# Parts of q and k kept in DRAM in the order of the contraction's rows, in a two-layer trunk of four mixers on one core

## The chip, the cores and the metric

The kernel runs on one core of one Trainium2 chip. A core has a matmul engine (PE, whose weight loads are listed as PEld), a vector engine (DVE), a scalar engine (ACT), a general one (POOL) and a queue of its own for transfers (SP, listed as SPq). Each engine works through its own list of instructions in order and waits at an instruction until everything that it needs is there. The transfers of SP are carried by 16 DMA engines. The metric is the time of the whole program on the device in microseconds (us); lower is better.

## The reference

One step of a hybrid trunk: DEPTH = 2 layers over 1024 latent tokens and 128 context tokens, width 1024. Cut to what the change touches:

```python
# in each layer: one input projection, four mixers, one output projection, then an MLP
nq, nk = rms_norm(heads(nq), g), rms_norm(heads(nk), g)           # 4 heads of 64
y_nat = nat_latent_attend(nq, nk, nv, nat_kc, nat_vc, rel_bias)   # windows of the 16 x 64 grid + 256 cached keys
dq, dk = rms_norm(halves(dq), g), rms_norm(halves(dk), g)         # 4 heads of 2 x 32
dq, k_all = axial_rope(dq), concat([diff_kc, axial_rope(dk)])     # 256 cached keys first
y_diff = rms_norm(softmax(q1 @ k1.T) @ v - lam * softmax(q2 @ k2.T) @ v)
mixed = concat([y_ssd, y_nat, y_rwkv, y_diff])
x = x + g1 * (mixed @ w_out)
x = x + g2 * (square(relu(norm(x) @ w_ff1)) @ w_ff2)
```

## The kernel before

Tokens lie along the free dimension: an activation is a tile of 128 features by T = 1152 tokens, and keys have 256 cached columns more (1408). Every matmul operand of the projections is split in two parts, `h` (rounded) and `l` (the rest), so that three products give the accuracy of float32. The scores of the attentions use the same split in one product: the contraction's rows hold the h part and the l part of the same features side by side.

A layer runs through these stages: norm and projections with the SSD mixer beside them; the projections of q and k (`proj_qk`) beside the first step of the RWKV mixer; the neighbourhood attention (`nat_core`) and then the differential attention (`diff_core`) beside the rest of RWKV; the output projection; the MLP. A scheduler orders the instructions of every engine when the program is built, by its own estimate of times, so an edit in one place can move instructions far from it.

In `split_to` the finished q or k of a chunk is copied to `qh` by ACT, the rest `ql` is taken by POOL, and SP writes both to a scratch tensor in DRAM: `nscr` for the neighbourhood attention, `dscr` for the differential one, both of shape [4 (q of two feature tiles, k of two), 2 parts, 128 features, 1408]. The tiles `qh` and `ql` have two buffers each, so the third write of a kind needs the first to have landed.

`nat_core` goes through four heads of 64 features. For each it fills `Q` (128 rows: 64 of part h, then 64 of part l) and two tiles `K0`, `K1` (128 rows each: 64 rows of one part of k, twice), with one transfer for every block of 64 rows: six transfers. `diff_core` goes through four heads, each of two halves; for each half `diff_operands` fills `Q` and `K` with one transfer for every block of 32 rows: four and four, the rows of Q being h, h, l, l and those of K h, l, h, l. All these tiles have one buffer for each tag, so the transfers for the next head wait until the last product `S` of the head before has read the tile, and the first `S` of the next head waits until they have landed. I call this place a head change; there are three in each attention of each layer, twelve in all. A ninth block of tokens (`b == 8`, the context) is the last of each head. What PE has to do between the two products is work of the block before (transposes at L1154, products with V at L1166) and of RWKV (L935 to L986).

Where `nat_core` begins, SP also carries the loads `vv`, `z` (the RWKV state) and the triangle blocks `Ti` to DRAM and back as `D`, and DVE has RWKV's short steps on `D` (L866 to L873) in the same list as the reading of the scores (L1279).

Of the kernel before, what the change touches and what calls it, by code (L numbers as in the profile page):

```python
# [8 lines left out]
F32 = mybir.dt.float32  # L9
# [8 lines left out]
NS, NP_ = 1024, 128  # L18
T = NS + NP_
# [11 lines left out]
def bcast_mid(ap, n):  # L31
    return ap.unsqueeze(1).to_broadcast([ap.shape[0], n, ap.shape[1]])
# [988 lines left out]

def split_to(env, tp, x, n, dst, c0, grid=False):

    nc = env.nc
    h = tp.tile([128, 384], F32R, tag="qh", name="qh", bufs=2)
    l = tp.tile([128, 384], F32R, tag="ql", name="ql", bufs=2)
    if grid:
        m = min(NS - c0, n)
        parts = [(by_columns(x[:, :m]), slice(0, m), lambda a: a.rearrange("p (b r c) -> p b r c", b=8, c=8))]
        if m < n:  # L1030
            parts.append((x[:, m:n], slice(m, n), lambda a: a))
        for xv, s, f in parts:
            nc.scalar.activation(out=f(h[:, s]), in_=xv, func=AF.Copy)
            nc.gpsimd.tensor_tensor(out=f(l[:, s]), in0=xv, in1=f(h[:, s].bitcast(F32)), op=ALU.subtract)
        g0 = c0 // 8
        for part, t in ((0, h), (1, l)):
            nc.sync.dma_start(out=dst[part][:, 0:NS].rearrange("p (b x) -> p b x", b=8)[:, :, g0:g0 + m // 8], in_=t[:, :m].bitcast(F32).rearrange("p (b x) -> p b x", b=8))
            if m < n:
                nc.sync.dma_start(out=dst[part][:, NS:T], in_=t[:, m:n].bitcast(F32))
        return  # L1040
    nc.scalar.activation(out=h[:, :n], in_=x, func=AF.Copy)
    nc.gpsimd.tensor_tensor(out=l[:, :n], in0=x, in1=h[:, :n].bitcast(F32), op=ALU.subtract)
    nc.sync.dma_start(out=dst[0][:, c0:c0 + n], in_=h[:, :n].bitcast(F32))
    nc.sync.dma_start(out=dst[1][:, c0:c0 + n], in_=l[:, :n].bitcast(F32))


class Steps:
# [87 lines left out]
    steps.add(last, turn, scale, *([] if rope is None else [rotate]))  # L1135


def cached_keys(env, tp, ck, scr):
    for t in range(2):
        x = tp.tile([128, 384], F32, tag="qx", name="cx", bufs=7)  # L1140
        env.nc.sync.dma_start(out=x[:, 0:256], in_=ck[t])
        split_to(env, tp, x[:, 0:256], 256, scr[2 + t], T)


def pv(env, sp, ps, e, kt, V, r0):
# [61 lines left out]
def nat_core(env, ps, pss, scr, vsrc, cv, nbias, yout, beside):  # L1207

    tc, nc, C = env.tc, env.nc, env.const
    with ExitStack() as ctx:  # L1210
        big = ctx.enter_context(tc.tile_pool(name="na_big", reuse_waits="tile", bufs=1, side="right"))
        sp = ctx.enter_context(tc.tile_pool(name="na_s", reuse_waits="tile", bufs=2, side="right"))
        behind, steps = Behind(), Steps()
# [16 lines left out]
        for h in range(4):  # L1230
            t, r0 = h // 2, (h % 2) * 64
            if h % 2 == 0:
                y = big.tile([128, T], F32, tag="y", name="nay", bufs=2)
            Q = sp.tile([128, T], F32R, tag="Q", name="Q", bufs=1)
            K = [sp.tile([128, T + 256], F32R, tag=f"K{i}", name=f"K{i}", bufs=1) for i in range(2)]

            for a in range(2):
                nc.sync.dma_start(out=Q[a * 64:a * 64 + 64].bitcast(F32), in_=scr[t, a, r0:r0 + 64, 0:T])
                for i in range(2):
                    nc.sync.dma_start(out=K[i][a * 64:a * 64 + 64].bitcast(F32), in_=scr[2 + t, i, r0:r0 + 64])  # L1240
            if r0 == 0:
                V = sp.tile([128, 11, 128], F32, tag="V", name="V", bufs=1)
                nc.sync.dma_start(out=V[:, 0:9], in_=vsrc[:, :, h * 64:h * 64 + 128])
                nc.sync.dma_start(out=V[:, 9:11], in_=cv[:, :, h * 64:h * 64 + 128])

            BT = sp.tile([128, 3, 16, 24], F32, tag="BT", name="BT", bufs=1)
            for m in range(3):
                nc.sync.dma_start(out=BT[:, m].rearrange("p a k -> p (a k)"), in_=nbias[:, m, :, h])
            BI = sp.tile([128, 9, 16, 8], F32, tag="BI", name="BI")
            nc.gpsimd.memset(BI[:, 2:4], 0.0)  # L1250
            for m, (o, i, n) in enumerate(((0, 1, 2), (4, 0, 2), (6, 0, 3))):
                nc.gpsimd.tensor_copy(BI[:, o:o + n], BT[:, m, :, i * 8:i * 8 + n * 8].rearrange("p a (b k) -> p b a k", b=n))
            flat = BI.rearrange("p b a k -> p (b a k)")
            if h == 1:
                beside()
            for b in range(NB):
                q = Q[:, b * 128:b * 128 + 128]

                if b == 8:
                    segs, kt = [([(NS, 128)], flat[:, 256:384])], [8]  # L1260
                elif b == 0:
                    segs, kt = [([(0, 256), (T, 256)], flat[:, 0:512])], [0, 1, 9, 10]
                elif b == 7:
                    segs, kt = [([(T, 256), (768, 256)], flat[:, 256:768])], [9, 10, 6, 7]
                else:
                    segs, kt = [([(b * 128 - 128, 384)], flat[:, 768:1152]), ([(T, 256)], flat[:, 256:512])], [b - 1, b, b + 1, 9, 10]
                kt = [(k, 128, i * 128) for i, k in enumerate(kt)]
                st = sp.tile([128, 8], F32, tag="st", name="st", bufs=4)
                e = sp.tile([128, 640], F32, tag="e", name="e", bufs=3)

                o = 0
                for i, (seg, bias) in enumerate(segs):
                    S = pss.tile([128, 512], F32, tag="s", name="S")
                    w = 0
                    for k0, n in seg:
                        nc.tensor.matmul(S[:, w:w + n], q, K[0][:, k0:k0 + n], start=True, stop=False)
                        nc.tensor.matmul(S[:, w:w + n], q, K[1][:, k0:k0 + n], start=False, stop=True)
                        w += n
                    nc.vector.tensor_tensor_reduce(out=e[:, o:o + w], in0=S[:, 0:w], in1=bias, op0=ALU.add, op1=ALU.min,  # L1279
                                                   scale=-1.0, scalar=st[:, 0:1] if i else 3e38, accum_out=st[:, i:i + 1])  # L1280
                    o += w
                nc.scalar.activation(out=e[:, 0:o], in_=e[:, 0:o], func=AF.Exp, scale=-1.0, bias=st[:, len(segs) - 1:len(segs)], accum_out=st[:, 4:5])
                nc.vector.reciprocal(out=rec[:, t, b, h % 2:h % 2 + 1], in_=st[:, 4:5])

                def values(b=b, h=h, e=e, kt=kt, V=V, y=y, r0=r0):
                    o = pv(env, sp, ps, e, kt, V, r0)
                    if b < 8:
                        nc.vector.tensor_copy(by_columns(y[r0:r0 + 64, 0:NS])[:, b], o.rearrange("p (r c) -> p r c", c=8))
                    else:
                        nc.vector.tensor_copy(y[r0:r0 + 64, NS:T], o)  # L1290
                    steps()
                    if r0 and b in (3, 7, 8):
                        steps.add(lambda: scale(h // 2, b // 4 * 4, 1 if b == 8 else 4, y))

                behind(values)
# [5 lines left out]
def diff_operands(env, pool, scr, j):  # L1301

    t, q0 = j // 4, (j % 4) * 32
    Q = pool.tile([128, T], F32R, tag=f"Q{j % 2}", name="Q", bufs=1)
    K = pool.tile([128, T + 256], F32R, tag=f"K{j % 2}", name="K", bufs=1)

    for a in range(2):
        for i in range(2):
            r = slice(a * 64 + i * 32, a * 64 + i * 32 + 32)
            env.nc.sync.dma_start(out=Q[r].bitcast(F32), in_=scr[t, a, q0:q0 + 32, 0:T])  # L1310
            env.nc.sync.dma_start(out=K[r].bitcast(F32), in_=scr[2 + t, i, q0:q0 + 32])
    return Q, K


# [111 lines left out]
def kernel(ctx: ExitStack, tc: tile.TileContext, A: dict, O: dict):  # L1426
    nc = tc.nc
    env = Env()
# [4 lines left out]
    def dram(shape):  # L1433
        cnt[0] += 1
        return tc.dram_tile(shape, F32, name=f"scr{cnt[0]}")
# [45 lines left out]
    for L in range(DEPTH):  # L1481
# [2 lines left out]
        zdt, nv, dv = dram([128, NB, 264]), dram([128, NB, 256]), dram([128, NB, 256])  # L1484
        Y = [dram([128, T]) for _ in range(6)]
        rscr = [dram([128, T]) for _ in range(13)]
        nscr, dscr, sk, nbias = dram([4, 2, 128, T + 256]), dram([4, 2, 128, T + 256]), dram([3, 8, 60, 24]), dram([16, 3, 8, 4, 384])
        scale_section(env, md, 1, ng[:, L, 0])
        env.wide = False

# [45 lines left out]
        with tc.tile_pool(name="qk", reuse_waits="tile", bufs=1, side="right") as qp:  # L1536
# [9 lines left out]
                nc.sync.dma_start(out=rope[i], in_=A["c_rope"][i])  # L1546
            steps = Steps()
            for t in range(4):
                proj_qk(env, qp, steps, WF[13 + t], H, pt[:, t:t + 1], 64, nscr[t], O["nat_k"][L, t - 2] if t > 1 else None)
            cached_keys(env, qp, A["nat_ck"][L], nscr)  # L1550
            for t in range(4):
                proj_qk(env, qp, steps, WF[17 + t], H, pt[:, 4 + t:5 + t], 32, dscr[t], O["diff_k"][L, t - 2] if t > 1 else None, rope)
            cached_keys(env, qp, A["diff_ck"][L], dscr)
            rwkv_join(env, u, 0, u00, psr)
            env.stg = qp
            proj_tm(env, A["w_in_tm"][L, 2], H, 256, dv, O["diff_v"][L], steps=steps)
# [218 lines left out]
```

## Time and profile before

| | |
|---|---|
| median of 3 runs | 4177.0 us (4174.42 to 4189.47) |
| profiled execution | 4174.25 us, its span 4172.5 us |
| PE busy | 3976.4 us, 95% of the span |
| PEld, DVE, ACT, POOL busy | 3688.6, 2479.1, 1499.7, 1122.7 us |
| mean granted clock of PE | 0.968 of 2.4 GHz |
| share of the 16 DMA engines' time in SP's transfers | 30.4% |

A busy engine is one that has an instruction under way; the granted clock is the share of its full speed that PE was given. The durations that the prediction uses come from the profiled execution, 2.75 us below the median.

### The profile page before, as it was taken

The numbers are of one execution on the slowest core, as the hardware profiler recorded it, in microseconds if no ns is written. First come the engines' busy times: TensorE is split into PE (matmuls) and PEld (weight loads), VectorE is DVE, ScalarE is ACT, GpSimd is POOL, SyncE is SP. The second block draws the span as 40 slices with busy tenths as digits, with TensorE's granted clock in tenths as the row PEclk, the third lists the DMA queues.
The fourth block names the chain that finished last, engine by engine and source line by source line (L and its number), as shares of the span: only waits on it lengthen the run. The fifth ranks groups of instructions, "written<-read, shape, count | busy, mean of one in ns | idle before, by whom it ended". The sixth has DMA issues, their size and how long they took to land.

```text
span 4172.5 us, 68251 instructions
## 1 busy us (share of the span) xinstructions
PE 3976.4 (95%) x26994; PEld 3688.6 (88%) x26994; DVE 2479.1 (59%) x5702; ACT 1499.7 (36%) x2872; POOL 1122.7 (27%) x874
## 2 busy tenths in 40 slices
PE   8899989989999999999999998899999999999999
PEld 5889877867889999999999997687777999999999
DVE  4897657678675994333356647577878363333333
ACT  4323325546643222111244233255567241111111
POOL 2234341123143211111133333302323331121111
PEclk9999989989999999999999999899999999999999
DMA  5654544323131551111135344533122201111112
GB/s 200 203 173 146 134 125 106 79 65 78 46 112 41 162 167 51 44 43 41 41 120 167 121 128 96 153 95 94 32 61 85 99 31 41 41 41 46 41 41 71
DMA packets 259598, 381.81 MB, mean 92 GB/s; under 512 B 123328, under 2 KB 193680, under 8 KB 258256
## 3 DMA queue, kind: packets, MB, share of 16 engines
q1 hardware_dynamic: 259216, 377.44, 30.4%
q8 instruction: 213, 3.49, 0.4%
q14 instruction: 105, 0.86, 0.1%
q0 software_dynamic: 64, 0.02, 0.0%
HBM read 288.43 MB, written 91.50 MB: 91 GB/s over the span
## 4 chain that ended last, share of the span: by engine, by line
PE 74%; DVE 12%; DMA 6%; issue 3%; ACT 2%; SPq 2%; POOL 1%; DVEq 0%; POOLq 0%; ACTq 0%
PE psd L101 12%; PE psd L99 12%; PE psd L100 12%; PE psx L101 5%; PE psx L99 5%; PE psx L100 5%; PE tps L1166 5%; PE tps L1154 2%; PE psd L943 1%; DVE tm L872 1%; PE S L1389 1%; DVE junk L162 1%; PE psd L935 1%; DMA mod<-in_w_mod_dram 1%; DMA Q<-scr 1%
## 5 line engine op out<-in xcount | busy, mean ns | idle before, releaser
L84 POOL TENSOR_TENSOR wl<-raw,wh 128x1024 fp32r<-128x1024 f32 (+3 forms) x200 | 480.0, 2401 | 1524.7 <-ACT wh L82 1513.1
L82 ACT ACTIVATE wh<-raw 128x1024 fp32r<-128x1024 f32 (+3 forms) x200 | 205.8, 1031 | 787.3 <-PE psd L101 667.5
L299 DVE SCALAR_TENSOR_TENSOR x<-psd,md,x 128x384 f32<-128x384 f32 (+2 forms) x442 | 212.7, 504 | 339.4 <-PE psd L101 339.0
L99 PE MATMUL psd<-fh,wl 128*128 128x384 f32 x992 | 334.8, 337 | 0.6 <-DVE s L382 0.6
L101 PE MATMUL psd<-fl,wh 128*128 128x384 f32 x992 | 335.3, 338 | 0.0
L100 PE MATMUL psd<-fh,wh 128*128 128x384 f32 x992 | 334.7, 337 | 0.0
L99 PE MATMUL psd<-h2h,wl 128*128 128x384 f32 x816 | 281.4, 345 | 6.1 <-ACT qx L1122 4.3
L100 PE MATMUL psd<-h2h,wh 128*128 128x384 f32 x816 | 279.4, 343 | 0.0
L101 PE MATMUL psd<-h2l,wh 128*128 128x384 f32 x816 | 278.2, 342 | 0.0
L1166 PE MATMUL tps<-pT,V 128*128 128x128 f32 x1920 | 265.8, 288 | 7.1 <-ACT pT L1161 6.0
L384 DVE TENSOR_TENSOR fl<-s,fh 128x384 fp32r<-128x384 f32 x192 | 207.1, 1079 | 97.4 <-ACT fh L383 97.0
L1166 PEld LDWEIGHTS tps<-pT,V 128*128 128x128 f32 x1920 | 242.1, 200 | 19.9 <-ACT pT L1161 8.2
L99 PE MATMUL psd<-h1h,wl 128*128 128x384 f32 x592 | 204.7, 346 | 8.4 <-ACT st L262 6.4
L99 PE MATMUL psd<-h0h,wl 128*128 128x384 f32 x592 | 206.7, 349 | 2.0 <-ACT st L262 2.0
L382 DVE SCALAR_TENSOR_TENSOR s<-psd,r 128x384 f32<-128x384 f32 x128 | 71.3, 557 | 229.5 <-ACT r L381 229.1
L100 PE MATMUL psd<-h0h,wh 128*128 128x384 f32 x592 | 204.1, 345 | 0.0
L100 PE MATMUL psd<-h1h,wh 128*128 128x384 f32 x592 | 203.8, 345 | 0.0
L101 PE MATMUL psd<-h0l,wh 128*128 128x384 f32 x592 | 203.7, 346 | 0.0
L101 PE MATMUL psd<-h1l,wh 128*128 128x384 f32 x592 | 203.3, 345 | 0.1
L1395 ACT ACTIVATE e<-e,st 128x1280 f32<-128x1280 f32 x144 | 180.6, 1254 | 62.5 <-DVE st L1394 54.2
L1161 ACT ACTIVATE pT<-tps 128x512 f32<-128x512 f32 (+2 forms) x336 | 153.4, 470 | 133.6 <-PE tps L1154 117.0
L299 DVE SCALAR_TENSOR_TENSOR x<-psx,md,x 128x384 f32<-128x384 f32 (+2 forms) x198 | 103.5, 538 | 163.5 <-PE psx L101 163.2
(614 smaller groups left out, 10918.2 us busy)
## 6 DMA issues: line engine op xcount, KB each, us to landing
raw<-in_w_ff_dram SPq DMA_DIRECT2D x128, 512.0 KB
mod<-in_w_mod_dram SPq DMA_DIRECT2D x80, 512.0 KB
raw<-in_w_in_fm_dram SPq DMA_DIRECT2D x42, 512.0 KB
scr<-st SPq DMA_DIRECT2D x78, 192.0 KB
scr<-x SPq DMA_DIRECT2D x26, 576.0 KB
K<-scr SPq DMA_DIRECT2D x32, 352.0 KB
K<-scr SPq DMA_DIRECT2D x64, 176.0 KB
u<-scr SPq DMA_DIRECT2D x18, 576.0 KB
```

The costliest lines, as they stand in the source:

```text
L82: nc.scalar.activation(out=h[:, :n], in_=raw, func=AF.Copy)
L84: nc.gpsimd.tensor_tensor(out=l[:, :n], in0=raw, in1=h[:, :n].bitcast(F32), op=ALU.subtract)
L99: nc.tensor.matmul(ps, al, bh, start=i == 0, stop=False)
L100: nc.tensor.matmul(ps, ah, bh, start=False, stop=False)
L101: nc.tensor.matmul(ps, ah, bl, start=False, stop=i == n - 1)
L299: env.nc.vector.scalar_tensor_tensor(out=x[:, kt, s0:s1], in0=ps[:, s0 - c0:s1 - c0], scalar=g[:, kt, cd:cd + 1], in1=x[:, kt, s0:s1], op0 ...
L382: nc.vector.scalar_tensor_tensor(out=s, in0=ps[:, :n], scalar=0.0, in1=r, op0=ALU.max, op1=ALU.mult)
L384: nc.vector.tensor_tensor(out=fl[j][:, c0:c0 + n], in0=s, in1=fh[j][:, c0:c0 + n].bitcast(F32), op=ALU.subtract)
L1154: nc.tensor.transpose(pp[0:n, i * 128:i * 128 + 128], e[:, o:o + n], C.ident)
L1161: nc.scalar.activation(out=pT[0:g[i][1], i * 128:j * 128], in_=pp[0:g[i][1], i * 128:j * 128], func=AF.Copy)
L1166: nc.tensor.matmul(out, V[0:n, vb], parts[k][0:n], start=k == 0, stop=k == len(kt) - 1)
L1395: nc.scalar.activation(out=e[:, :N], in_=e[:, :N], func=AF.Exp, scale=-1.0, bias=m, accum_out=st[:, 6:7] if c else s0)
```

## The change

The scratch tensors get a new order. `nscr` becomes [4, 128 features, 2 parts, 1408], `dscr` [4, 128 features, 4, 1408]. In `dscr` each part is written twice, next to each other or alternating (q: h, h, l, l; k: h, l, h, l), by one transfer with the source repeated. The rows of a feature then lie in the order in which they are contracted, and `Q` and `K` are each filled by one transfer of 128 rows, in the order feature, part. In `nat_core` the repetition of k's rows is made by the transfer itself. The products, their sizes and their number stay as they are; the order of the rows in a contraction changes for Q and K alike.

```diff
@@ split_to
-        for part, t in ((0, h), (1, l)):
-            nc.sync.dma_start(out=dst[part][:, 0:NS].rearrange("p (b x) -> p b x", b=8)[:, :, g0:g0 + m // 8], in_=t[:, :m].bitcast(F32).rearrange("p (b x) -> p b x", b=8))
+        for d, t in zip(dst, (h, l)):
+            nc.sync.dma_start(out=d[:, 0, 0:NS].rearrange("p (b x) -> p b x", b=8)[:, :, g0:g0 + m // 8], in_=t[:, :m].bitcast(F32).rearrange("p (b x) -> p b x", b=8))
...
-    nc.sync.dma_start(out=dst[0][:, c0:c0 + n], in_=h[:, :n].bitcast(F32))
-    nc.sync.dma_start(out=dst[1][:, c0:c0 + n], in_=l[:, :n].bitcast(F32))
+    for d, t in zip(dst, (h, l)):
+        m = d.shape[1]
+        src = t[:, :n].bitcast(F32)
+        nc.sync.dma_start(out=d[:, :, c0:c0 + n] if m > 1 else d[:, 0, c0:c0 + n], in_=bcast_mid(src, m) if m > 1 else src)
+
+
+def nat_parts(scr, t):
+
+    return scr[t, :, 0:1], scr[t, :, 1:2]
+
+
+def diff_parts(scr, t):
+
+    s = scr[t] if t < 2 else scr[t].rearrange("p (a b) x -> p b a x", a=2)
+    return (s[:, 0:2], s[:, 2:4]) if t < 2 else (s[:, 0], s[:, 1])
@@ nat_core
-            for a in range(2):
-                nc.sync.dma_start(out=Q[a * 64:a * 64 + 64].bitcast(F32), in_=scr[t, a, r0:r0 + 64, 0:T])
-                for i in range(2):
-                    nc.sync.dma_start(out=K[i][a * 64:a * 64 + 64].bitcast(F32), in_=scr[2 + t, i, r0:r0 + 64])
+            nc.sync.dma_start(out=Q.bitcast(F32), in_=scr[t, r0:r0 + 64, :, 0:T].rearrange("f a x -> (f a) x"))
+            for i in range(2):
+                nc.sync.dma_start(out=K[i].bitcast(F32), in_=scr[2 + t, r0:r0 + 64, i].unsqueeze(1).to_broadcast([64, 2, T + 256]))
@@ diff_operands
-    for a in range(2):
-        for i in range(2):
-            r = slice(a * 64 + i * 32, a * 64 + i * 32 + 32)
-            env.nc.sync.dma_start(out=Q[r].bitcast(F32), in_=scr[t, a, q0:q0 + 32, 0:T])
-            env.nc.sync.dma_start(out=K[r].bitcast(F32), in_=scr[2 + t, i, q0:q0 + 32])
+    for X, s, n in ((Q, t, T), (K, 2 + t, T + 256)):
+        env.nc.sync.dma_start(out=X.bitcast(F32), in_=scr[s, q0:q0 + 32, :, 0:n].rearrange("f a x -> (f a) x"))
@@ tile_hybrid_trunk_kernel
-        nscr, dscr, sk, nbias = dram([4, 2, 128, T + 256]), dram([4, 2, 128, T + 256]), dram([3, 8, 60, 24]), dram([16, 3, 8, 4, 384])
+        nscr, dscr, sk, nbias = dram([4, 128, 2, T + 256]), dram([4, 128, 4, T + 256]), dram([3, 8, 60, 24]), dram([16, 3, 8, 4, 384])
```

The callers pass `nat_parts(nscr, t)` or `diff_parts(dscr, t)` where they passed `nscr[t]` or `dscr[t]`. Lines of the new kernel are a few numbers higher (the product S at L1389 is L1398 there).

The scheduler's order differs from the first writes to `dscr` on, in every list of both layers up to the output projection. On SP, where `nat_core` begins in layer 0 (scr_234 is nscr, scr_235 dscr, z_5993 and z_6585 the two states that RWKV needs first), there stood:

```order
L1240 DMA K_8570<-scr_234 64x1408
L1240 DMA K_8571<-scr_234 64x1408
L715 DMA vv<-scr_228 128x1152
L917 DMA z_5993<-in_st_rwkv_dram 128x64
L1238 DMA Q<-scr_234 64x1152
L1240 DMA K_8570<-scr_234 64x1408
L1240 DMA K_8571<-scr_234 64x1408
L1243 DMA V<-scr_213 128x9x128
L1244 DMA V<-in_nat_cv_dram 128x2x128
L1248 DMA BT<-scr_237 128x1x384
L917 DMA z_6585<-in_st_rwkv_dram 128x64
```

Behind these rows SP had two more BT, seven of the eight loads of the first differential half, the two writes of `Ti`, the third z, the eighth load and only then the load of `D`. At the same place there now stands:

```order
L1253 DMA K_8570<-scr_234 128x1x1408
L1253 DMA K_8571<-scr_234 128x1x1408
L1256 DMA V<-scr_213 128x9x128
L1257 DMA V<-in_nat_cv_dram 128x2x128
L715 DMA vv<-scr_228 128x1152
L917 DMA z_5993<-in_st_rwkv_dram 128x64
L1261 DMA BT<-scr_237 128x1x384 x3
L1320 DMA Q<-scr_235 128x1152
L1320 DMA K<-scr_235 128x1408
L917 DMA z_6585<-in_st_rwkv_dram 128x64
L861 DMA scr_5851<-Ti 32x36x32 x2
L917 DMA z_7430<-in_st_rwkv_dram 128x64
```

The load of `D` is the next row. The whole operands and V moved ahead of the first z, and two transfers stand where eight stood ahead of `Ti` and `D`.

On PE, at the last head change of `diff_core` in layer 1 (the first row is the previous head's last product of the first half, the single 128x128 row further down that of the second half; the 128x512 and 128x256 rows are the next head's first products), there stood:

```order
L1389 MATMUL S<-K,Q 128x128
L963 MATMUL psd<-E,R_24967 128x128 x8
L1166 MATMUL tps<-pT,V 128x128 x10
L1389 MATMUL S<-K,Q 128x128
L984 MATMUL psx<-st_24921,E 64x64
L984 MATMUL psx<-st_24924,E 64x64
L986 MATMUL psx<-E,st_24921 64x64
L986 MATMUL psx<-E,st_24924 64x64
L1154 MATMUL tps<-pack,e 128x128 x6
L1389 MATMUL S<-K,Q 128x512
L1389 MATMUL S<-K,Q 128x256
L1389 MATMUL S<-K,Q 128x512
```

And now, with the last product of the first half five rows above the first row shown (four small ones of L984 and L986 lie between):

```order
L957 MATMUL psd<-R_24907,Ti 64x128 x8
L1168 MATMUL tps<-pack,e 128x128 x6
L1398 MATMUL S<-K,Q 128x128
L984 MATMUL psx<-st_24861,E 64x64
L984 MATMUL psx<-st_24864,E 64x64
L986 MATMUL psx<-E,st_24861 64x64
L986 MATMUL psx<-E,st_24864 64x64
L963 MATMUL psd<-E,R_24907 128x128 x8
L1168 MATMUL tps<-pack,e 128x128 x4
L1180 MATMUL tps<-pT,V 128x128 x10
L1398 MATMUL S<-K,Q 128x512
L1398 MATMUL S<-K,Q 128x256
```

Between the last product of the first half and the next head's first product the list had L963, L1166, four small products and six transposes; it now has eight small products, L957, ten transposes in two groups, L963 and L1180.

## Rows read from the trace of the kernel before

**Rows 1.** The page: each engine's busy time (share of the span), instructions.

```profile
PE 3976.4 (95%) x26994; PEld 3688.6 (88%) x26994; DVE 2479.1 (59%) x5702; ACT 1499.7 (36%) x2872; POOL 1122.7 (27%) x874
```

**Rows 2.** Waits of the matmul engine on S: us in total, times, longest.

```profile
PE S L1389 <- issue: 5.6, 3, 2.7
...
PE S L1276 <- issue: 4.1, 2, 3.1
...
PE S L1277 <- DMA K<-scr: 3.4, 3, 1.3
...
PE S L1389 <- DMA Q<-scr: 3.3, 2, 1.8
...
PE S L1276 <- DMA K<-scr: 2.0, 2, 1.6
```

**Rows 3.** Timeline of SP's queue at the last head change of layer 1.

```profile
3164.34 0.31 SPq L1310 DMA_DIRECT2D Q<-scr  x1
...
3167.48 0.42 SPq L1311 DMA_DIRECT2D K<-scr  x1
```

**Rows 4.** Timeline of matmuls there; [idle before, releaser].

```profile
3164.14 2.00 PE L963 MATMUL psd<-E,R 128*128 128x128 f32 x16
3165.98 2.40 PE L1166 MATMUL tps<-pT,V 128*128 128x128 f32 x20
...
3169.03 1.08 PE L1154 MATMUL tps<-pack,e 128*128 128x128 f32 x6 [0.21 <-ACT pT L1161]
3172.83 0.81 PE L1389 MATMUL S<-K,Q 128*128 128x512 f32 x3 [2.73 <-issue]
```

**Rows 5.** Window: stretch, length, busy us by engine (count), clock, DMA share, GB/s.

```profile
1042.00:1051.00 9.00, 9.00 (x39) 7.47 (x37) 3.50 (x15) 2.10 (x4) 0.00 (x0) 0.50 0.21 42
```

**Rows 6.** Windows at the start of the neighbourhood attention, layers 0 and 1.

```profile
616.00:653.00 37.00, 20.08 (x171) 16.33 (x170) 17.96 (x49) 7.51 (x16) 16.70 (x38) 0.72 0.85 199
2666.00:2704.00 38.00, 24.36 (x209) 19.41 (x208) 20.19 (x56) 9.58 (x20) 16.64 (x38) 0.82 0.85 197
```

**Rows 7.** Timeline of SP's queue there, layer 0.

```profile
626.72 0.34 SPq L917 DMA_DIRECT2D z<-in_st_rwkv_dram  x1
...
643.57 0.31 SPq L865 DMA_DIRECT2D D<-scr  x1
```

**Rows 8.** Timeline of DVE there, layer 0.

```profile
635.86 0.52 DVE L920 TENSOR_SCALAR st<-z,sc 64x64 f32<-64x64 f32 x2 [5.73 <-DMA z<-in_st_rwkv_dram]
...
647.16 0.09 DVE L866 MEMSET D<- 72x32 f32 x1 [7.94 <-DMA D<-scr]
```

**Rows 9.** Timeline of matmuls there, layer 0.

```profile
637.16 0.33 PE L952 MATMUL psd<-R,E 64*64 64x64 f32 x2 [2.75 <-DVE E L944]
...
647.77 0.58 PE L1276 MATMUL S<-K,Q 128*128 128x256 f32 x1 [6.02 <-DVE st L1279]
```

**Rows 10.** Issues: transfer, queue, operation, count, KB each.

```profile
K<-scr SPq DMA_DIRECT2D x32, 352.0 KB
...
K<-scr SPq DMA_DIRECT2D x64, 176.0 KB
...
scr<-qh SPq DMA_DIRECT2D x40, 192.0 KB
```

**Rows 11.** Windows with one kind of transfer in flight.

```profile
734.00:737.00 3.00, 3.00 (x47) 2.69 (x47) 1.58 (x7) 2.30 (x8) 1.12 (x3) 1.00 1.05 215
963.00:967.00 4.00, 3.85 (x30) 3.32 (x29) 4.00 (x8) 1.94 (x6) 1.32 (x1) 1.00 1.03 215
729.00:731.00 2.00, 2.00 (x17) 1.70 (x18) 0.92 (x4) 0.31 (x1) 2.00 (x1) 1.00 1.05 340
610.00:612.00 2.00, 1.64 (x14) 1.54 (x14) 0.00 (x0) 0.68 (x3) 0.79 (x2) 1.00 1.00 359
```

**Rows 12.** Window of layer 0's projections of q and k.

```profile
570.00:617.00 47.00, 45.47 (x319) 39.75 (x317) 24.91 (x55) 18.07 (x40) 23.50 (x23) 1.00 0.53 175
```

**Rows 13.** Timeline of ACT in that window.

```profile
604.10 0.38 ACT L282 ACTIVATE st<-psd 128x256 f32<-128x256 f32 x1 [4.36 <-POOL ql L1042]
```

More of the change, by code (lines that the diff above doesn't have):

```diff
@@ L1035, in split_to @@
         g0 = c0 // 8
-        for part, t in ((0, h), (1, l)):
-            nc.sync.dma_start(out=dst[part][:, 0:NS].rearrange("p (b x) -> p b x", b=8)[:, :, g0:g0 + m // 8], in_=t[:, :m].bitcast(F32).rearrange("p (b x) -> p b x", b=8))
+        for d, t in zip(dst, (h, l)):
+            nc.sync.dma_start(out=d[:, 0, 0:NS].rearrange("p (b x) -> p b x", b=8)[:, :, g0:g0 + m // 8], in_=t[:, :m].bitcast(F32).rearrange("p (b x) -> p b x", b=8))
             if m < n:
-                nc.sync.dma_start(out=dst[part][:, NS:T], in_=t[:, m:n].bitcast(F32))
+                nc.sync.dma_start(out=d[:, 0, NS:T], in_=t[:, m:n].bitcast(F32))
         return
@@ L1135, in proj_qk, with cached_keys @@
     steps.add(last, turn, scale, *([] if rope is None else [rotate]))
-def cached_keys(env, tp, ck, scr):
+def cached_keys(env, tp, ck, scr, parts):
     for t in range(2):
@@ L1141, in cached_keys @@
         env.nc.sync.dma_start(out=x[:, 0:256], in_=ck[t])
-        split_to(env, tp, x[:, 0:256], 256, scr[2 + t], T)
+        split_to(env, tp, x[:, 0:256], 256, parts(scr, 2 + t), T)
 def pv(env, sp, ps, e, kt, V, r0):
@@ L1548 @@
             for t in range(4):
-                proj_qk(env, qp, steps, WF[13 + t], H, pt[:, t:t + 1], 64, nscr[t], O["nat_k"][L, t - 2] if t > 1 else None)
-            cached_keys(env, qp, A["nat_ck"][L], nscr)
+                proj_qk(env, qp, steps, WF[13 + t], H, pt[:, t:t + 1], 64, nat_parts(nscr, t), O["nat_k"][L, t - 2] if t > 1 else None)
+            cached_keys(env, qp, A["nat_ck"][L], nscr, nat_parts)
             for t in range(4):
-                proj_qk(env, qp, steps, WF[17 + t], H, pt[:, 4 + t:5 + t], 32, dscr[t], O["diff_k"][L, t - 2] if t > 1 else None, rope)
-            cached_keys(env, qp, A["diff_ck"][L], dscr)
+                proj_qk(env, qp, steps, WF[17 + t], H, pt[:, 4 + t:5 + t], 32, diff_parts(dscr, t), O["diff_k"][L, t - 2] if t > 1 else None, rope)
+            cached_keys(env, qp, A["diff_ck"][L], dscr, diff_parts)
             rwkv_join(env, u, 0, u00, psr)
```

## The prediction

> **What bounds the kernel now.** I read the page's engine line first: PE is busy in 3976.4 of the span's 4172.5 us, the next engine in 59% of it [rows 1]. The list of matmuls, their sizes and their number stay, so the change can only return time in which PE stands still (196 us, both ends of the program included) or runs at a granted clock below 1.00, and it can only cost by adding to these. Two places touch the edit: the twelve head changes and the start of the neighbourhood attention.
>
> **The head changes.** The second view was the list of PE's waits, for those that end at a product S. Five groups of it are held by the loads of Q and K ("issue" is what the profile says where it names no releaser; I count it here because of the timeline below): 5.6 + 4.1 + 3.4 + 3.3 + 2.0 = 18.4 us in 12 waits [rows 2]. The timelines of one head change show the race. The first half's eight loads are issued from 3164.34 to 3167.9 [rows 3]; PE works on other things for about 5.9 us (L963 2.00, L1166 2.40, six transposes 1.08, small products) and then stands still for 2.73 until 3172.83 [rows 4]. So the set takes 8.5 us from the first issue to its use. It holds four K blocks of 176 KB and four Q blocks of 1152/1408 of that [rows 10], 1.31 MB. In the windows in which only such loads are in flight, 64-row ones of the neighbourhood attention and 32-row ones of the differential one, the DMA engines are busy all the time (share 1.03 to 1.05) and move 215 GB/s [rows 11]; 1.31 MB takes 6.1 us by that, and 2.4 of the 8.5 are the first issue, the landing and the wake-up.
>
> Behind a long wait the clock falls too: after one head change of layer 0, PE is busy for 9.0 of 9.0 us at a granted clock of 0.50, so 4.5 us of that stretch are lost to the lower level of 1.2 GHz [rows 5].
>
> **The start of the neighbourhood attention.** In layer 0's 37 us PE is busy in 20.08 at a mean clock of 0.72, in layer 1's 38 us in 24.36 at 0.82, and the DMA share is 0.85 in both [rows 6]. Here the queue is the resource: z is issued at 626.72 behind the operands of the first two heads, D at 643.57 behind seven loads of the first differential half and both writes of Ti [rows 7]. DVE stands still for 5.73 us for z and for 7.94 for D [rows 8], and with it PE, which needs DVE's E and DVE's reading of S: 2.75 and 6.02 us [rows 9].
>
> **The change, part by part.**
>
> *Fewer, wider loads.* Q and K need 56 transfers where they needed 176 (per layer 4 heads of 3 for 6, and 8 halves of 2 for 8). The bytes are the same. Each issue holds SP's queue 0.3 to 0.4 us [rows 3], but SP's issues run faster than the engines drain them, so I give the 120 missing issues nothing by themselves. What counts is the rate. The transfers of 128 rows in this trace move 340 GB/s (a load of whole tiles) and 359 (writes, the projections' results) [rows 11]; those of 64 and 32 rows 215. I take 340 for the new loads, since they are loads of the same kind of row, 4.6 and 5.6 KB long in DRAM; below stands the case in which the rate does not come from the row count. Then 1.31 MB takes 3.9 us and the set 3.9 + 2.4 = 6.3 in place of 8.5; a neighbourhood head (four K of 352 KB, two Q, 2.03 MB) takes 6.0 + 2.4 = 8.4 in place of 11.8.
>
> The new order gives PE 8.5 us of other work at the place quoted, by the prices of [rows 4] (L963 2.00, L1180 2.40, ten transposes 1.8, L957 and eight small products 2.3, which I set from the same kinds of instruction there). Counted in the same way, the five other changes of the differential attention have 6.8 to 9.0 us, all more than 6.3; the six of the neighbourhood attention have 6.7 to 10.0 against 8.4, and at two of them another load stands ahead. That leaves about 3 us. **First term: 3 − 18 = −15 us**; bounds 0 (each wait replaced by one for something else, since S is only one of several things that come late there) and −18.
>
> The Trainium skill, "SBUF — State Buffer", section "Can I just issue two DMAs to hit both halves?", says that the ports are picked by a single transfer's span of partitions, and its table gives 8 of 16 ports and some 218 GB/s for 64 rows or fewer, 436 for 128. This trace agrees with the first (215) and shows 340 to 359, not 436, for the second. By 436 the set would take an estimated 5.4 us, and the first term would be nearer −17 than −15.
>
> *The clock.* Where PE no longer stands still it keeps full speed. The stretch of [rows 5] is worth 4.5; I have not counted every such stretch as belonging to a head change, and the new order keeps some waits of other causes ahead of them. **Second term: −5**; bounds 0 and −15 (about three such stretches).
>
> *The start.* The queue's first part now has the whole operands ahead of the first z: that one comes late by about 2 us. The second z and D have less ahead of them: seven 32-row loads of 1.13 MB or so at 215 (5.3 us) become two of 1.31 MB at 340 (3.9), the first heads' operands come 3 to 4 us earlier, and the writes of Ti no longer stand behind them. I put D's landing at about 641, and with it DVE's L866 6 us earlier than 647.16 [rows 8]. Other waits of the stretch, for the last writes of the projections, stay, so not all of this reaches PE: of 2.75 + 6.02 [rows 9] I take 4 us in each layer. **Third term: −8**; bounds 0 (the first z late eats it) and −14.
>
> *The wider writes.* Every h and l part of the differential q and k is written twice in one transfer: in a layer 4 x 3 chunks x 2 parts x 192 KB [rows 10] and 2 x 2 of 128 KB for the cached keys, 5.2 MB more, at 359 GB/s 14.6 us of transfer in each layer. They fall into a stretch with a DMA share of 0.53, in which PE is busy for 45.47 of 47 us [rows 12]; 22 us of the DMA engines' time are free there, which is the cover. Without it the price would be 29 us in both layers. It is not a clean cover: `qh` and `ql` have two buffers, POOL waits for the landing of an earlier write, and ACT, with st<-psd behind, stood still 4.36 us for POOL's ql [rows 13]. A transfer of twice the bytes lands about 0.5 us later. Late next would be ACT's emptying of PSUM, and then PE. **Fourth term: +4** (2 in each layer); bounds 0 and +29.
>
> **Sum.** −15 − 5 − 8 + 4 = −24 us against the profiled 4174.25: 4150; the median lies 2.75 above the profiled execution, so **4153 us**.
>
> **The rivals.**
> *The waits are only replaced (no change).* Against −24 stands that S is not late by much at any one place (the longest 3.1 us), that ACT's exponentials and DVE's readings follow S, and that the scheduler reordered PE's list too: what it puts behind S earlier can wait for itself. If half of the first and third terms comes back as other waits and the clock gives nothing: −7 − 4 + 4 = −7, so 4170.
> *Everything that the start and the head changes lose comes back.* All half-speed stretches behind them vanish as well: −18 − 15 − 14 + 2 = −45, so 4132. For it speaks the clock of 0.72 and 0.82 [rows 6]; against it that most of these idle times have several causes.
> *Slower: the rate does not come from the row count.* If the row order in DRAM or the repeated source rows of K keep the new loads at 215 GB/s or less, each set is still 6.1 us, but it is one Q and one K, and the first S, which needs part of the columns of both, gets neither early; at 8.5 us against work of 6.8 to 9.0 the waits would about stay (+0), and at the neighbourhood changes, 11.8 against 6.7 to 10.0, grow to some 18 us for six; the first z is 6 us later and D no earlier; with the half-speed stretches behind longer waits (+10) and the writes (+4) this gives about +30, so 4207. It decides below some 250 GB/s, where a neighbourhood head takes 8.1 + 2.4 = 10.5 us. Against it speaks every 128-row row of [rows 11].
> *The doubled writes find no cover.* +29 against −28: 4178, which I count with no change.
>
> **How the numbers follow.** A difference under 0.5% (21 us) is about what a measurement of this kernel can't tell from none: faster means below 4156, slower above 4198. I give the forecast 0.42 (its own range 4140 to 4163, so that a third of it falls into no change), all comes back 0.12, waits replaced or writes bare 0.37, slower 0.09, of which a little stays under 0.5%. Faster: 0.28 + 0.12 + 0.05 of the cases between = 0.45; slower 0.08; the rest, 0.47, within 0.5%. The range leaves out the low end of the large gain and most of the slower case: 4130 to 4185.
>
> **What would show it.** Right: windows with only Q and K loads in flight near 340 GB/s; the five groups of waits on S for Q, K or "issue" sum to about 3 us; DVE's wait for D at L866 well under 7.94; the half-speed stretch behind the head change near 1042 gone; ACT's and POOL's waits for writes in the projections a little longer, PE there as busy as before. Wrong: the window rate stays near 215; or it rises, the waits on S vanish, and PE's total idle time does not fall, because the waits stand at L1154 (for ACT's pT), L1166 or RWKV's products; or the projections' stretch grows by more than 10 us a layer.

## The result and the profile after

| | before | after |
|---|---|---|
| median | 4183.24 us (4174.42 to 4190.02, 4 runs) | 4131.85 us (4128.52 to 4136.58, 4 runs) |
| profiled execution, its span | 4174.25 us, 4172.5 us | 4136.58 us, 4134.5 us |
| PE busy, not busy in the span | 3976.4 us, 196.1 us | 3974.1 us, 160.4 us |

The ratio is 0.988, with a 95% interval of 0.9865 to 0.9894: 50 us faster. A second set of runs of the same kernel, further down, gave 0.9872 (0.9851 to 0.9893). The direction and the range held; the gain is twice the forecast.

The page's engine line (engine, busy time, share, instructions) shows where it is not: in the two profiled executions PE does the same work in the same time.

```profile
PE 3974.1 (96%) x26994; PEld 3687.3 (89%) x26994; DVE 2474.9 (60%) x5702; ACT 1497.1 (36%) x2872; POOL 1117.7 (27%) x874
```

The waits of PE that end at a product S, for transfers (total, times, longest), answer to [rows 2]:

```profile
PE S L1289 <- DMA K<-scr: 10.8, 2, 6.3
...
PE S L1289 <- DMA Q<-scr: 1.7, 1, 1.7
...
PE S L1398 <- DMA K<-scr: 0.4, 1, 0.4
```

The 10.8 us are no head change: they are the first S of `nat_core` in each layer. In the kernel before PE's list had L850 ahead of this S, and PE stood there for DVE's A instead; in the change the first S stands ahead of L850. Two of the twelve waits of [rows 2], in the kernel before, belong to this place too, since they are layer 1's first products of `nat_core`:

```profile
2679.20 0.55 PE L1276 MATMUL S<-K,Q 128*128 128x256 f32 x1 [0.43 <-DMA K<-scr]
2680.93 0.39 PE L1277 MATMUL S<-K,Q 128*128 128x256 f32 x1 [1.18 <-DMA K<-scr]
```

So the waits at the head changes were 18.4 − 1.6 = 16.8 us, and what is left of them is 1.7 + 0.4 = 2.1.

The last head change of layer 1, SP's queue and then the matmuls, answers to [rows 3, 4]:

```profile
3131.25 0.33 SPq L1320 DMA_DIRECT2D Q<-scr  x1
...
3133.37 0.32 SPq L1320 DMA_DIRECT2D Q<-scr  x1
```

```profile
3134.85 2.05 PE L963 MATMUL psd<-E,R 128*128 128x128 f32 x16 [0.16 <-ACT R L959]
...
3139.33 0.59 PE L1398 MATMUL S<-K,Q 128*128 128x512 f32 x2
```

The first half's two loads start at 3131.25, the second half's at 3133.37. PE comes to the next head's first S at 3139.33, after the work that the order put there, and does not wait. Windows with Q and K in flight (a load of RWKV's k is issued behind them at 721.38 and at 837.88), of the neighbourhood and the differential attention (length, busy us of PE, PEld, DVE, ACT and POOL, clock, DMA share, GB/s), answer to the 215 GB/s of [rows 11]:

```profile
719.00:723.00 4.00, 3.92 (x43) 3.20 (x40) 3.64 (x7) 1.93 (x5) 1.09 (x1) 1.00 0.99 391
835.00:838.00 3.00, 1.26 (x12) 1.07 (x10) 1.52 (x2) 0.00 (x0) 0.00 (x0) 1.00 1.01 412
```

At the start of `nat_core`, the windows of both layers, DVE's and PE's timelines answer to [rows 6, 8, 9]:

```profile
612.00:643.00 31.00, 20.66 (x195) 16.94 (x194) 15.69 (x39) 6.23 (x14) 15.68 (x36) 0.83 0.82 248
2640.00:2672.00 32.00, 21.30 (x176) 16.37 (x175) 17.57 (x46) 6.51 (x14) 16.48 (x38) 0.68 0.79 227
```

```profile
634.75 0.52 DVE L920 TENSOR_SCALAR st<-z,sc 64x64 f32<-64x64 f32 x2 [2.13 <-DMA z<-in_st_rwkv_dram]
...
639.77 0.52 DVE L1292 CUSTOM_DVE_ANT_0 e<-S,BI 128x384 f32<-128x384 f32 x1 [2.13 <-issue]
639.79 0.09 DVE L866 MEMSET D<- 72x32 f32 x1
```

```profile
622.16 0.87 PE L1289 MATMUL S<-K,Q 128*128 128x256 f32 x2 [6.29 <-DMA K<-scr]
623.63 3.57 PE L850 MATMUL psr<-A,B 64*64 64x64 f32 x64 [0.60 <-DVE A L830]
...
636.05 1.02 PE L952 MATMUL psd<-R,E 64*64 64x64 f32 x14 [2.76 <-DVE E L944]
```

PE is not busy in 10.3 and 10.7 us of these windows, where it was 16.9 and 13.6; the comparison is rough, since the windows do not hold the same matmuls (195 and 176 here, 171 and 209 there). The second z is waited for 2.13 us instead of 5.73, and L866 runs at 639.79 instead of 647.16. The profile names no wait for D, but DVE stands still for 2.13 us without a named releaser just ahead of L866, which runs 3.5 us after D's issue at 636.30, as it ran 3.6 us after it in the kernel before: by this, D is probably still waited for, some 2 us instead of 7.94:

```profile
636.30 0.31 SPq L865 DMA_DIRECT2D D<-scr  x1
```

The 2.76 for E is still there, and a wait of 6.29 for the first K is new. It and the 0.60 for A behind it stand where layer 0 of the kernel before had one wait for A:

```profile
624.15 3.68 PE L850 MATMUL psr<-A,B 64*64 64x64 f32 x64 [7.76 <-DVE A L830]
```

### The profile page after: what moved, and what is told of

The parts are those of the page before. It is cut to its first block, busy times and chain, and to the rows that moved or that the text cites. A ratio compares the mean times of both kernels' runs of the same rounds, so it can differ in the third digit from the quotient of the medians.

```text
span 4134.5 us, 68047 instructions
## 1 busy us (share of the span) xinstructions
PE 3974.1 (96%) x26994; PEld 3687.3 (89%) x26994; DVE 2474.9 (60%) x5702; ACT 1497.1 (36%) x2872; POOL 1117.7 (27%) x874
## 4 chain that ended last, share of the span: by engine, by line
PE 71%; DVE 8%; DMA 2%; issue 2%; ACT 2%; POOL 1%; SPq 1%; DVEq 0%; ACTq 0%; POOLq 0%
PE psd L101 11%; PE psd L99 11%; PE psd L100 11%; PE psx L101 5%; PE psx L99 5%; PE psx L100 5%; PE tps L1180 5%; PE tps L1168 2%; PE psd L943 2%; PE S L1398 2%; PE psd L935 1%; DVE tm L872 1%; PE psd L963 1%; PE psx L984 1%; PE psd L952 1%
## 5 line engine op out<-in xcount | busy, mean ns | idle before, releaser
L1180 PE MATMUL tps<-pT,V 128*128 128x128 f32 x1920 | 257.2, 282 | 0.6 <-ACT pT L1175 0.5
L1180 PEld LDWEIGHTS tps<-pT,V 128*128 128x128 f32 x1920 | 234.2, 194 | 10.8 <-issue 1.7
```

Source lines behind the costliest of these rows:

```text
L1180: nc.tensor.matmul(out, V[0:n, vb], parts[k][0:n], start=k == 0, stop=k == len(kt) - 1)
```

## The experiments

**The theories.** Mine: 128-row transfers move faster, so operands land before PE needs them. First rival: every edit makes the scheduler draw a new order, and this draw is a lucky one. Second rival: it is the number of transfers, not their width. All variants draw an order of their own; what is common to those with narrow loads, and to those with whole ones, is the effect of the loads. All times are medians; ratios are to the kernel before on the same chip, with their intervals.

**Whole tiles cut in two** (storage and writes of the change):

```diff
-        env.nc.sync.dma_start(out=X..., in_=scr[s, q0:q0 + 32, :, 0:n]...)
+        for a in range(2):   # nat_core's Q and K in the same way
+            f0 = q0 + a * 16
+            env.nc.sync.dma_start(out=X[a * 64:a * 64 + 64]..., in_=scr[s, f0:f0 + 16, :, 0:n]...)
```

> The new storage and the wider writes stay; each Q and K is loaded by two transfers of 64 rows (112 transfers in all, where the change has 56 and the kernel before 176). If the gain comes from the rate of 128-row transfers, the windows with only such loads in flight show about 215 GB/s, PE waits for Q or K at S for 10 to 18 us in all, and the ratio to the kernel before is 0.994 to 1.000. If it comes from fewer transfers or from the order in which the operands stand, the ratio is near the change's 0.988 whatever the rate.

4179.47 us, 0.9994 (0.9976 to 1.0012): the whole gain is gone. Two windows of its loads, and PE's waits at S:

```profile
677.00:682.00 5.00, 5.00 (x35) 3.84 (x34) 4.94 (x13) 3.68 (x9) 1.16 (x2) 1.00 1.04 217
1048.00:1052.00 4.00, 2.61 (x25) 2.08 (x24) 1.77 (x6) 1.95 (x4) 0.83 (x1) 1.00 1.04 217
```

```profile
PE S L1402 <- DMA K<-scr: 20.2, 7, 6.7
...
PE S L1292 <- DMA K<-scr: 4.2, 4, 1.5
...
PE S L1291 <- issue: 2.1, 2, 1.5
...
PE S L1291 <- DMA K<-scr: 1.9, 2, 1.2
```

217 GB/s at a full DMA share, and 28.4 us of waits. The count of transfers had fallen from 176 to 112 and brought nothing: the second rival falls.

**The loads as before, storage and wider writes of the change**; and **the same with single writes**:

```diff
+            for a in range(2):   # first variant; diff_core's loads by 32 rows as before
+                nc.sync.dma_start(out=Q[a * 64:a * 64 + 64]..., in_=scr[t, r0:r0 + 64, a, 0:T])
...
-dram([4, 128, 4, T + 256])   # second variant, besides
+dram([4, 128, 2, T + 256])
```

> The new storage and the wider writes, but the loads as before: 176 transfers of 64 and 32 rows. By the rate nothing is gained and the wider writes cost their 4 us: ratio 1.000 to 1.004, waits on S for Q or K near 18 us, load windows near 215 GB/s. If the storage or the new order of instructions by itself brings the gain, 0.988 to 0.994.

> The new interleaved storage with single writes and the narrow loads as before (176 transfers). Against the variant with wider writes and narrow loads (1.0037) it isolates the wider writes: 0.995 to 1.001 if they cost some 4 to 30 us, the same 1.004 if they are hidden. If the interleaved rows in DRAM alone made transfers faster, the load windows would show more than 215 GB/s; I expect 215.

4194.87 us, 1.0037 (1.0016 to 1.0057), and 4186.92 us, 1.0016 (0.9996 to 1.0036). The storage by itself brings nothing; a window of the first variant's loads:

```profile
677.00:681.00 4.00, 4.00 (x31) 2.60 (x31) 2.63 (x9) 1.89 (x5) 1.40 (x4) 1.00 1.01 211
```

The two differ by 0.2%, with intervals that overlap.

**Order alone.** K's transfers ahead of Q's, in the change and in the kernel before:

```diff
-    for X, s, n in ((Q, t, T), (K, 2 + t, T + 256)):
+    for X, s, n in ((K, 2 + t, T + 256), (Q, t, T)):
```

> The change with the transfers of K ahead of Q, nothing else; the order of PE's instructions differs from the change's in many places. If the order as such is worth little, the ratio is 0.986 to 0.990; if the order drawn by the scheduler is worth tens of us, it leaves that band.

> The kernel before with each K transfer issued ahead of its Q; storage, sizes, counts and rates are the same, only the scheduler draws another order. If the order as such is worth little, ratio 0.997 to 1.003 with waits on S for Q or K near 18 us. In the variants so far PE's waits at the transposes and products with V came to 10 to 17 us where the kernel before has 26, narrow loads or not; if that is a peculiarity of the order of the kernel before, it falls here too. If it comes from the storage or the wider writes, it stays near 26.

4139.72 us, 0.9903 (0.9873 to 0.9934), and 4180.57 us, 0.9991 (0.9971 to 1.0011). A new order alone moves the time by 0.1 to 0.3% in these two pairs; all the orders with narrow loads lie between 0.9991 and 1.0037, none near 0.988. So the first rival falls. In the change with K first, PE's waits at S and at L850:

```profile
PE psr L850 <- DVE A L830: 7.8, 1, 7.8
...
PE psx L850 <- DVE A L830: 6.1, 1, 6.1
...
PE S L1398 <- DMA Q<-scr: 1.4, 2, 0.7
```

In this order the first S of `nat_core` stands behind L850 again, and PE stands at L850 for DVE's A, 7.8 + 6.1, as in the kernel before. The stretch without work at the start is there in both orders; only the line that it shows at differs.

**One attention at a time:**

> Only the neighbourhood attention has the new storage and the 128-row loads; the differential one is as before, with single writes. By the transfer rate its six head changes lose their waits (9.5 us of the 18.4) and the start of the stage gets its first operands and D sooner, so 12 to 20 us less: ratio 0.995 to 0.997. If the gain were a matter of the order alone, it would not split between the two parts: either one could show all of it or none.

> Only the differential attention has the new storage, the wider writes and the 128-row loads. By the transfer rate its head changes lose 8.9 us of waits and D has two transfers ahead of it in place of eight; the wider writes take back some 4 us: ratio 0.994 to 0.998. Both parts together should come to the change's 0.988 within 0.3%.

Neighbourhood attention alone (the change in `nat_parts`, `nat_core` and `nscr`): 4148.24 us, 0.9926 (0.9905 to 0.9946), more than I expected. Differential alone: 4170.43 us, 0.9975 (0.9954 to 0.9996). Together 0.0074 + 0.0025 = 0.0099, against 0.012 to 0.013 for the change, inside the intervals. Most of the waits stand in the part that stays narrow; first the neighbourhood variant (L1288 is its product in `nat_core`, the first of the stage again; L1400 that of `diff_core`), then the differential one (L1290 and L1291 are `nat_core`, L1399 `diff_core`):

```profile
PE S L1288 <- DMA K<-scr: 11.6, 2, 6.5
...
PE S L1400 <- DMA K<-scr: 7.8, 3, 3.2
...
PE S L1400 <- issue: 4.8, 2, 4.4
```

```profile
PE psr L850 <- DVE A L830: 7.8, 1, 7.8
...
PE psx L850 <- DVE A L830: 6.1, 1, 6.1
...
PE S L1290 <- DMA K<-scr: 5.3, 3, 3.3
...
PE S L1290 <- issue: 4.6, 1, 4.6
...
PE S L1399 <- DMA K<-scr: 3.6, 3, 1.5
...
PE S L1291 <- DMA K<-scr: 3.2, 3, 1.4
```

The 3.6 us at L1399 are head changes with whole loads: there the order decides too, by how much other work it puts between the two products.

**The start alone taken back**, head changes whole:

```diff
+            if h == 0:      # and j == 0 in diff_operands: 64-row halves, as in the first variant
...
+            else:           # the change's transfers
```

> As the change, but the first neighbourhood head and the first differential half of each layer are loaded by two transfers of 64 rows for each tile. This takes back the effect on the start of the stage alone. If the third term is right, 8 to 11 us are lost: ratio 0.990 to 0.991, with DVE's wait for D back and no waits for Q or K at the other head changes. If the start is worth nothing, 0.988.

4148.01 us, 0.9907 (0.9879 to 0.9936). DVE's waits for the second z and D are back, beside 2.13 and some 2 us in the change:

```profile
640.08 0.52 DVE L920 TENSOR_SCALAR st<-z,sc 64x64 f32<-64x64 f32 x2 [5.79 <-DMA z<-in_st_rwkv_dram]
...
651.67 0.09 DVE L866 MEMSET D<- 72x32 f32 x1 [7.59 <-DMA D<-scr]
```

The medians stand 16 us apart and the ratios 0.003, which is 11 to 15 us; the intervals overlap, so the size is rough, while the place is shown by DVE's waits. In the profile PE is not busy for 166.8 us, beside 160.4 and 163.5 in the two profiles of the change, and the mean clock is the same: 3 to 6 us of the loss are seen there, the rest stays open.

**The wider writes taken away.** First both parts written once and both loads repeating rows, then q alone:

```diff
+    q = scr[t, 2 * q0:2 * q0 + 64, 0:T].unsqueeze(1).to_broadcast([64, 2, T])
+    k = scr[2 + t, 2 * q0:2 * q0 + 64].unsqueeze(0).to_broadcast([2, 64, T + 256])   # second variant: k as in the change
```

> The 128-row loads stay, but each part of the differential q and k is written once, and the load repeats the rows (as the change does for K of the neighbourhood attention); 10.5 MB of writes less in both layers. If the wider writes cost what I took (4 us), the ratio is 0.986 to 0.988; if nothing covers them (29 us), 0.981; if they are free, as the change, 0.988. Loads should still move about 390 GB/s.

> As the change, but the parts of the differential q are written once and repeated by the load, with 64 source rows as the outer count; k is still written twice. 2.4 MB of writes less in each layer, 6.6 us of transfer time by the rate of the writes. If the wider writes are hidden, as the change: 0.986 to 0.990; if they are bare, about 13 us less: 0.985. The load of Q reads each row of DRAM twice and should still move about 390 GB/s, other than K in the variant with an outer count of two.

> The change itself once more beside the next kernel, to have more executions of it: ratio 0.987 to 0.990, mean granted clock about 0.968 against 0.964 of the kernel before.

> The variant with the parts of the differential q written once, against the change itself on the same chip: 6.6 us of write time less in each layer. If the wider writes are hidden, the two times agree within 0.2%; if they are bare, this one is 0.3% faster.

The first took 4319.12 us, 1.0334 (1.0297 to 1.0372), and says nothing of the writes: its K load, with an outer count of 2, is far slower. A window with that load in flight, and PE's wait:

```profile
1075.00:1081.00 6.00, 0.00 (x0) 0.00 (x0) 0.00 (x0) 0.00 (x0) 0.00 (x0) 0.74 0.13 53
```

```profile
PE S L1398 <- DMA K<-scr: 128.4, 12, 14.0
```

A DMA share of 0.13 is that of two of sixteen engines, at 53 GB/s. The second variant's Q, whose outer count is 64, moves at full rate though it reads every row twice (a window in which its Q and K are in flight):

```profile
1021.00:1024.00 3.00, 3.00 (x29) 3.00 (x28) 1.84 (x8) 1.27 (x5) 0.83 (x1) 1.00 1.02 420
```

It took 4135.57 us, 0.9889 (0.9848 to 0.9929), and in the second set 4138.96 us, 0.9894 (0.9875 to 0.9913), beside 4131.56 us, 0.9872 (0.9851 to 0.9893), for the change itself. Fewer written bytes did not make it faster, so no variant beats the change.

**All runs side by side.** Of each profile I add up PE's waits of three kinds, from the same view: at S for a transfer or "issue", at L850 for A, and at the transposes and products with V (`tps`). "Not busy" is the span less PE's busy time, whatever the cause, from the page. The clock is the mean of the granted clocks of all timed executions.

```
kernel                      ratio          S      A    tps    sum  not busy   clock
before                      1             18.4   13.9  26.4   58.7     196.1   0.964
before, K first             0.9991        24.7   13.9  15.8   54.4     195.0   0.964
storage only                1.0016        20.0   13.9  20.3   54.2     191.9   0.962
storage, wider writes       1.0037        26.8   13.9  13.8   54.5     190.4   0.960
tiles in two halves         0.9994        28.4   13.9  16.9   59.2     192.6   0.963
differential only           0.9975        16.7   13.9  13.9   44.5     178.2   0.965
neighbourhood only          0.9926        24.9    0.6  12.2   37.7     176.2   0.967
start in halves             0.9907         3.2   13.9  13.3   30.4     166.8   0.969
change, K first             0.9903         1.4   13.9  16.4   31.7     165.2   0.968
change, q written once      0.9889        12.9    0.0  13.7   26.6     158.0   0.968
change                      0.988         12.9    1.3  13.4   27.6     160.4   0.969
```

Five orders with narrow loads have 54 to 59 us of such waits, spread differently over the kinds; the four with whole loads at all head changes have 27 to 32 (the second profiles of the change and of q written once have 27.2 and 22.9). Whatever the kinds, PE is not busy for 190 to 196 us in the first five and for 158 to 167 in the last four.

## Why the prediction was right, and where its size was off

**The rate** (the step on which all rests): right in kind, low in size. I took 340 GB/s; whole loads moved 391 and 412 in the windows above and 420 in the variant with q once. Width decides it: the same rows from the same storage in halves moved 217. The table of the Trainium skill that I set against it, "SBUF — State Buffer", section "Door 1: The DMA port swizzle (why `[64,N]` ≈ `[32,N]`)", gives 436 GB/s for 128 rows and some 218 for 32 and for 64 (less for fewer). The trace agrees with the latter (215, and 217 in halves) and stands nearer to 436 than to my 340.

**First term** (−15 at the head changes): 16.8 became 2.1, so −15. I had read the 18.4 as twelve waits at head changes; two of them, 1.6 us, are the start of layer 1's `nat_core`. And I had put the bound at −18, the sum of the waits that the profile lays on Q, K or "issue" at S. The table suggests that this was not all that late operands cost: with narrow loads the waits at S and at the transposes and products with V came to 40 to 45 us in every one of the five orders, though each order split them differently, and in the change they came to 26, of which 10.8 stand at the start, where the kernel before waited at L850. All three kinds together fell by 31. That the waits at the products behind are an after-effect of the same late S is argued from these sums, not shown for a single instruction.

**Third term** (−8 at the start): PE's idle time in the windows fell by 6.6 + 2.9 = 9.5. L866 runs at 639.79; I had said 641. Taking the wide loads away from the start alone costs some 11 us or more by the times, of which the profile shows 3 to 6, and brings both of DVE's waits back.

**Second term** (−5 for the clock) is mis-sized too. In the two profiled executions it does not show at all, because their mean clocks are 0.968 and 0.967: the profile that I read was, by its clock, one of the best executions of the kernel before. Of 67 executions of that kernel beside these experiments four have 0.968, with 4172.4 us in the mean; all have 4181.7 us and 0.9639. Of the change eight have 4131.8 us and 0.9688. Among the 67, the time falls by 3.0 us for every 0.001 of clock (correlation −0.85), so 0.0049 is worth an estimated 15 us. The pages bear this out, since PE's list holds the same products everywhere: it is busy for 4002.8 us at 0.959 (storage, wider writes), 3992.6 at 0.963 (before, K first), 3976.4 at 0.968 (before) and 3967.5 at 0.969 (the change's second profile).

The traces also show where the clock is lost. I count PE's busy time times (1 − granted clock) in windows of 10 us. In the two attentions (from the stretch in which PE stands ahead of the first S or L850 to the last S) it comes to 57 us in the profile before, to 72, 76, 81 and 88 in the other four with narrow loads, and to 49 to 60 in the six profiles with whole loads at the head changes. In all the rest of the program it is 55 to 59 with narrow loads and 54 to 66 with whole ones. So the clock that the change gives back is in the attentions, and the profile before was an execution that had lost little there. The one stretch that I had priced is gone as well: from 880 to 1100 us every window of 20 us has a clock of 1.00, among them:

```profile
1040.00:1060.00 20.00, 19.20 (x169) 15.61 (x169) 16.35 (x47) 14.14 (x25) 3.59 (x2) 1.00 0.09 25
```

**The sum.** My terms without the clock were −15 − 8 + 4 = −19 us; PE's time without work fell from 196.1 to 160.4, by 36 (to 163.5, by 33, in the second profile). For the clock I had −5, where the estimate is −15. Together −48 to −51, beside the 50 us between the means of 4181.7 and 4131.8. So the mechanism was right, and both of its parts were sized too small, the time without work by about 15 us and the clock by about 10. That the result still fell into the range, close to its lower end, owes something to the width of the range.

**Fourth term** (+4 for the wider writes): hardly seen. POOL waited 12.2 us for writes of ql in the whole program where it waited 13.5, ACT now 8.5 for writes of qh, but in the window that answers to [rows 12] the DMA share is 0.76 and PE is busy in 44.25 of 47 us, where it was in 45.47:

```profile
568.00:615.00 47.00, 44.25 (x300) 38.57 (x299) 23.09 (x54) 17.09 (x38) 21.54 (x20) 0.93 0.76 255
```

Halving the extra writes gave no gain in two sets, adding them to narrow loads cost 0.2% with overlapping intervals. What stays open is a cost between nothing and, by the two medians, some 9 us.

**The rivals.** "The waits are only replaced" fell: replacement exists (6.29 for K at the start, in L850's place), but the sums of the three kinds halve and all of PE's time without work falls by 33 to 36 us. "The rate does not come from the row count" fell with the tiles in two halves. "Everything comes back" is nearest in size (4132), with other addends than I gave it, so the nearness is partly luck: half-speed stretches did not all vanish (the start has clocks of 0.83 and 0.68), and the idle time away from the head changes brought more.

## What to carry to other kernels

Where operands are reloaded into single buffers, compare the width of the loads first: here transfers of 64 rows moved 211 to 217 GB/s and transfers of 128 rows 391 to 420, while fewer transfers (112 for 176) and the storage order brought nothing by themselves. The waits that the profile laid on the late loads (18 us) were less than what came back when the loads were no longer late (33 to 36 us without work), and a new order moved waits from one line to another; so add up the kinds before pricing. Before pricing a clock loss from one profile, see where that execution's mean clock lies among several runs.

## What the runs showed of the hardware that was not expected

A transfer whose outermost count is 2 (rows repeated twice as a whole) kept the sixteen DMA engines at a share of 0.13, that of two of them: 53 GB/s, 128.4 us of waits, where the same repetition inside an outer count of 64 moved 420 GB/s. The Trainium skill says this: "DMA: Bandwidth & Descriptors", section "Rules for kernel authors", has the number of engines set by the slowest dimension and names a leading repetition as the case; the trace agrees. The 67 executions of one unchanged kernel differed in mean granted clock between 0.958 and 0.968, and some 70% of the spread of their times goes with it (0.85 squared).
